# A hybrid attention trunk on one core: context rows, denominators and key preparation moved within a pair of heads

## Chip, cores and metric

The kernel runs on one NeuronCore of a Trainium2 chip. The metric is the device time of one execution in microseconds (us). TensorE is written PE, VectorE DVE, ScalarE ACT, GpSimd POOL, SyncE SP.

## What is computed

One inference step of a two-layer backbone over 128 context tokens and 512 latent tokens, together T = 640 columns. Each layer normalises its input, modulates it, projects it, and gives it to three mixers: A (grouped-query attention, 8 heads), B (latent attention with compressed keys and a rope part, 8 heads), C (a linear scan). Each mixer's output is multiplied by a gate, projected, merged and projected out. The change touches A and B alone. What they compute, cut from the reference:

```python
def _block_attention(q, k, v):
    s = jnp.einsum('bqkgd,bskd->bkgqs', q_blk, k) * scale
    p = jax.nn.softmax(s, axis=-1)
    return jnp.einsum('bkgqs,bskd->bqkgd', p, v)

ya = _block_attention(q, k, v) * jax.nn.silu(a_z)
yb = _mla_attend(qb, ckv, b_kr, lp) * jax.nn.silu(b_z)
```

Context tokens attend to the 128 context tokens. Latent tokens attend to 512 latent and 128 cached keys.

## The kernel before

All matrices are float32. Where accuracy asks for it, an operand is split into a high part (ACT copies it to a rounded type) and a low part (DVE subtracts; POOL does it for weights during the attention), and a product becomes two or three matmuls. `split` (L163, L164) does this for every tile; so its lines stand for many operations, told apart by tile names.

In each layer the stage before the attention runs mixer C with the first projections; the stage behind it merges the three branches (`merge`, products `pm` at L178 to L180) and projects out. The attention works through eight pairs of heads, 0 to 3 of A and 4 to 7 of B. For one pair:

- `context` (L911 on): scores `scc` of the 128 context rows for both heads (L920), maximum, exponential into `Pc` with the row sums.
- `head` for each of the two heads. Scores: for each of four query tiles, `sc` (L958), a maximum `nm` (L961), an exponential `P` (L963) whose row sums go to `rsum`. Values: for each of five key tiles, four transposes `pp` of P (L973), the split into `ph` and `pl`, two products into `po` (L977, L978). Then `finish` adds the two halves of `po` into `OT`: a copy on ACT (L908), an addition on DVE (L909).
- `context2`: transposes `ppc` of `Pc`, split, products `poc` (L939, L940), `finish`.
- `pair_out` (L982 on): reciprocal `ri` of the row sums (L987), broadcast `rib` on POOL (L989), five transposes `pri` (L993), `OT` times `pri` on DVE reading PSUM (L995), `OT` times the gate tile `z` on POOL (L996), and the store (L997).

Meanwhile `pump` advances a generator, `stream(i)`, 18 times in a pair, by a rate from the hand-written table `PLAN`, and `drain` plays the rest of it at the pair's end. The stream prepares the next pair (for B: `b_pair` with queries `QT` and, for every second pair, the projection of the rope queries; `b_pair2` with the rope queries `QR`, transposes `pqr` at L1149, and the values `VS`, products `pvb`; `b_head` with the keys `KH`, `KL` of one head, products `pkh`) and holds the projection of this pair's `z` (`gate_z`, products `pcm` at L225 to L227, 48 for a tile unless it was made earlier and is loaded) and gate projections that are left over (`units`). Before the change, the keys of the second head of a B pair are made at the start of that pair, ahead of its stream.

PSUM has two score buffers of two banks each (tag `S`, also used by `pkh`), two banks of tag `pt` (`pp`, `scc`, `ppc`, `pri`), one of `po` and one of `f`. The tile framework inserts the semaphores and orders the instructions of each engine ahead of time (`schedule_with_timeline_sim=True`): program order is its priority, and what it finds ready earlier may go ahead. Each engine then executes its own list in order. SP issues all loads and stores in its own order.

Of the kernel before, what the change touches and what calls it, by code (L numbers as in the profile page):

```python
# [20 lines left out]
KT = 8  # L21
# [86 lines left out]
class Trunk:  # L108
# [834 lines left out]
    def head(self, e, h, ps, rate):  # L943

        V, S, PE, sm, split, ap = self.V, self.S, self.PE, self.sm, self.split, self.ap
        ident = self.ident
        kq, VS = e.keys[h], e.VS(h)
        OT, rsum = e.OT, e.rsum


        Ps = []
        for qt in range(4):
# [13 lines left out]
            self.pump(rate)  # L966


        po = ps.tile([128, 512], F32, tag="po", name="po")
        for t in range(5):  # L970
            p = ps.tile([128, 512], F32, tag="pt", name="pp")
            for qt in range(4):
                PE.transpose(p[:, qt * 128:(qt + 1) * 128], Ps[qt][:, t * 128:(t + 1) * 128], ident)  # L973
            ph = ap.tile([128, 512], F32R, tag="ph", name="ph", bufs=2)
            pl = ap.tile([128, 512], F32R, tag="pl", name="pl", bufs=2)
            split(ph, pl, p)
            PE.matmul(po, lhsT=VS[:, 1 + t, :], rhs=ph, start=(t == 0), stop=False)  # L977
            PE.matmul(po, lhsT=VS[:, 1 + t, :], rhs=pl, start=False, stop=(t == 4))  # L978
            self.pump(rate)
        self.finish(po, h, OT[:, 128:640])  # L980

    def pair_out(self, e, dst, ps):  # L982

        V, PE = self.V, self.PE
        OT = e.OT
        ri = self.sm.tile([128, 10], F32, tag="ri", name="ri")
        V.reciprocal(out=ri, in_=e.rsum.rearrange("p t h -> p (t h)"))  # L987
        rb = self.tq([128, 5, 2, 64], "rib")
        self.G.tensor_copy(out=rb.rearrange("p t h d -> p (t h) d"), in_=ri.unsqueeze(2).to_broadcast([128, 10, 64]))  # L989
        for t0, n in ((0, 4), (4, 1)):  # L990
            p = ps.tile([128, 512], F32, tag="pt", name="pri")
            for j in range(n):
                PE.transpose(p[:, j * 128:(j + 1) * 128], rb[:, t0 + j].rearrange("p h d -> p (h d)"), self.ident)  # L993
            ts_ = slice(t0 * 128, (t0 + n) * 128)
            V.tensor_tensor(out=OT[:, ts_], in0=OT[:, ts_], in1=p[:, 0:n * 128], op=ALU.mult)  # L995
        self.G.tensor_tensor(out=OT, in0=OT, in1=e.z, op=ALU.mult)  # L996
# [8 lines left out]
    def a_keys(self, l, wp, gp, ps, fill):  # L1005
# [5 lines left out]
        self.KT = KTt = self.kp.tile([128, 2, 2, 768], F32R, tag="KT", name="KT")  # L1011
# [21 lines left out]
        for j, src in enumerate((f32(khr), klo)):  # L1033
            for t0, n in ((0, 4), (4, 2)):
# [3 lines left out]
                for g in range(2):  # L1038
                    for c in range(2):
                        S.copy(out=KTt[c * 64:c * 64 + 64, g, j, t0 * 128:(t0 + n) * 128],  # L1040
# [584 lines left out]
```

## Time and profile before

| | us |
|---|---|
| median of 3 runs | 2320.77 |
| lowest and highest | 2318.45, 2337.36 |
| the profiled execution | 2325.66 |
| its span, first to last instruction | 2323.9 |

The profile is of one execution. Its durations sum to the span, and the execution's own time is 1.8 us longer. In rows of a timeline the first number is the start in us from the span's start and the second the duration in us. A bracket at a row's end holds the engine's idle time just before it and what ended it. A row of windows gives the stretch, its width, the busy time of PE, PEld, DVE, ACT and POOL with the number of instructions, PEclk, the DMA share and GB/s. PEld is PE's weight loading. PEclk is the granted share of the TensorE clock: 1.00 is 2.4 GHz, 0.50 is 1.2 GHz, and a value between them is the mean over a stretch.

### The profile page before, as it was taken

How to read it: one execution, taken by the hardware profiler on the slowest of the kernel's cores; microseconds unless marked ns; L12 is line 12 of the kernel's file. 1: busy time of each engine (PE TensorE's matmuls, PEld its weight loads, DVE VectorE, ACT ScalarE, POOL GpSimd, SP SyncE). 2: the span in 40 equal slices, each digit the busy share in tenths (PEclk: the TensorE clock that was granted, in tenths of full speed). 3: DMA queues.
4: the chain of work that ended last, by engine and by line, in shares of the span. 5: the costliest groups of instructions: out<-in, count | busy, mean ns of one | idle time of the engine just before them, and what ended most of it. 6: DMA issues, size and time to landing. Idle time of an engine off the chain costs nothing.

```text
span 2323.9 us, 40367 instructions
## 1 busy us (share of the span) xinstructions
PE 2130.8 (92%) x15380; PEld 2016.8 (87%) x15380; DVE 1589.3 (68%) x3062; ACT 1108.1 (48%) x2462; POOL 690.2 (30%) x761
## 2 busy tenths in 40 slices
PE   8899998999789889989989999999898889999898
PEld 6889998998789778879988999999898777888898
DVE  4676877867845676775648668668677568667673
ACT  4444443544443666662354444434443447667333
POOL 3332527335233221102033133253352332210011
PEclk9999989989899999999999999899797999999899
DMA  6232222222223311126612322222123231110562
GB/s 227 77 102 77 78 73 95 73 93 84 88 91 109 100 38 52 39 77 192 200 53 74 102 73 79 76 94 76 58 74 99 67 101 46 46 55 24 174 191 83
DMA packets 111762, 209.70 MB, mean 90 GB/s; under 512 B 14416, under 2 KB 33488, under 8 KB 111568
## 3 DMA queue, kind: packets, MB, share of 16 engines
q1 hardware_dynamic: 111568, 207.12, 28.1%
q8 instruction: 121, 1.98, 0.4%
q14 instruction: 73, 0.60, 0.1%
HBM read 163.52 MB, written 43.55 MB: 89 GB/s over the span
## 4 chain that ended last, share of the span: by engine, by line
PE 65%; DVE 18%; ACT 7%; DMA 4%; issue 4%; POOL 2%; DVEq 0%; SPq 0%; ACTq 0%; POOLq 0%
PE pcm L225 10%; PE pcm L226 10%; PE pcm L227 10%; PE sc L958 3%; PE sca L767 2%; PE pm L178 2%; PE pm L179 2%; PE pm L180 2%; DVE wlo L175 2%; PE pA L611 2%; PE pp L973 2%; PE px L679 1%; DVE nm L961 1%; PE scb L782 1%; ACT whi L174 1%
## 5 line engine op out<-in xcount | busy, mean ns | idle before, releaser
L225 PE MATMUL pcm<-hh,whi 128*128 128x320 f32 x1952 | 636.0, 326 | 21.7 <-DVE modc L252 6.7
L227 PE MATMUL pcm<-hh,wlo 128*128 128x320 f32 x1952 | 626.1, 321 | 13.7 <-DVE wlo L175 13.6
L226 PE MATMUL pcm<-hl,whi 128*128 128x320 f32 x1952 | 625.9, 321 | 0.0
L225 PEld LDWEIGHTS pcm<-hh,whi 128*128 128x128 f32 x1952 | 381.3, 195 | 29.4 <-DVE modc L252 7.9
L227 PEld LDWEIGHTS pcm<-hh,wlo 128*128 128x128 f32 x1952 | 380.2, 195 | 18.0 <-DVE wlo L175 16.9
L174 ACT CAST whi<-wraw 128x512 fp32r<-128x512 f32 (+1 forms) x356 | 226.6, 666 | 331.3 <-PE pcm L226 122.0
L226 PEld LDWEIGHTS pcm<-hl,whi 128*128 128x128 f32 x1952 | 381.5, 195 | 1.5
L175 DVE TENSOR_TENSOR wlo<-wraw,whi 128x512 fp32r<-128x512 f32 (+1 forms) x262 | 224.4, 871 | 95.1 <-ACT whi L174 91.3
L175 POOL TENSOR_TENSOR wlo<-wraw,whi 128x512 fp32r<-128x512 f32 x94 | 124.1, 1337 | 195.1 <-ACT whi L174 171.1
L778 POOL COPY ubd<-VZ 64x128 f32<-64x128 f32 x160 | 68.0, 425 | 328.1 <-ACT VZ L775 291.1
L164 DVE TENSOR_TENSOR pl<-pp,ph 128x512 fp32r<-128x512 f32 x160 | 108.4, 685 | 47.8 <-ACT ph L163 46.7
L178 PE MATMUL pm<-yh,whi 128*128 128x320 f32 x384 | 121.7, 317 | 7.1 <-DVE OT L995 3.0
L163 ACT CAST ph<-pp 128x512 fp32r<-128x512 f32 x160 | 92.4, 587 | 64.5 <-PE pp L973 53.9
L961 DVE TENSOR_REDUCE nm<-sc 128x1 f32<-128x640 f32 x128 | 104.4, 818 | 25.0 <-PE sc L958 23.6
L179 PE MATMUL pm<-yl,whi 128*128 128x320 f32 x384 | 121.3, 316 | 0.0
L180 PE MATMUL pm<-yh,wlo 128*128 128x320 f32 x384 | 121.0, 315 | 0.0
L963 ACT ACTIVATE P<-sc,nm 128x640 f32<-128x640 f32 x128 | 102.0, 798 | 18.7 <-DVE nm L961 14.4
L973 PE MATMUL pp<-small,P 128*128 128x128 f32 x640 | 102.2, 280 | 7.2 <-ACT P L963 4.3
L973 PEld LDWEIGHTS pp<-small,P 128*128 128x128 f32 x640 | 80.9, 144 | 24.9 <-ACT P L963 5.3
L611 PE MATMUL pA<-L,BK 128*128 128x128 f32 x640 | 90.7, 285 | 11.4 <-ACT AB L616 7.8
L767 PE MATMUL sca<-VZ,L 128*128 128x64 f32 x640 | 93.3, 285 | 7.7 <-DVE VZ L799 7.6
L996 POOL TENSOR_TENSOR OT<-OT,z 128x640 f32<-128x640 f32 x16 | 27.8, 1736 | 239.7 <-DVE OT L995 216.2
(375 smaller groups left out, 5021.6 us busy)
## 6 DMA issues: line engine op xcount, KB each, us to landing
wraw<-in_win SPq DMA_DIRECT2D x156, 256.0 KB, 2.9
wraw<-in_wg SPq DMA_DIRECT2D x96, 256.0 KB, 3.1
wraw<-in_wmod SPq DMA_DIRECT2D x64, 256.0 KB, 2.9
gsp<-gt SPq DMA_DIRECT2D x48, 320.0 KB, 3.1
gt<-gsp SPq DMA_DIRECT2D x48, 320.0 KB, 3.4
wraw<-in_wo SPq DMA_DIRECT2D x24, 512.0 KB, 4.4
cm<-gsl SPq DMA_DIRECT2D x26, 320.0 KB, 2.5
wraw<-in_wmod SPq DMA_DIRECT2D x16, 512.0 KB, 6.5
```

The costliest lines, as they stand in the source:

```text
L174: self.S.copy(out=hi[part], in_=raw)
L175: sub.tensor_tensor(out=lo[part], in0=raw, in1=f32(hi[part]), op=ALU.subtract)
L178: self.PE.matmul(out, lhsT=lh, rhs=rh, start=first, stop=False)
L179: self.PE.matmul(out, lhsT=lh, rhs=rl, start=False, stop=False)
L180: self.PE.matmul(out, lhsT=ll, rhs=rh, start=False, stop=last)
L225: PE.matmul(p[0:m, 0:H], lhsT=wh[:, kt], rhs=self.hh[:, kt, rs], start=(kt == 0), stop=False)
L226: PE.matmul(p[0:m, 0:H], lhsT=wh[:, kt], rhs=self.hl[:, kt, rs], start=False, stop=False)
L227: PE.matmul(p[0:m, 0:H], lhsT=wl[:, kt], rhs=self.hh[:, kt, rs], start=False, stop=(kt == KT - 1))
L611: PE.matmul(pA[:, j * 128:(j + 1) * 128], lhsT=BK[:, u].rearrange("p a s -> p (a s)"), rhs=L1[h][:, u].rearrange("p a s -> p (a s)"), star ...
L767: PE.matmul(a4[:, d, h], lhsT=L1[h][:, uu[d]].rearrange("p a s -> p (a s)"), rhs=VZ[h][:, cc[d], :], start=(h == 0 and d == 0), stop=False ...
L961: V.tensor_reduce(out=nm, in_=sc[:, :, 0:H], axis=AX.XY, op=ALU.max, negate=True)
L973: PE.transpose(p[:, qt * 128:(qt + 1) * 128], Ps[qt][:, t * 128:(t + 1) * 128], ident)
```

## The change

- `head` becomes `scores` and `values`. `context2` now stands between the scores and the values of the first head. The reciprocals with `rib` and the `pri` transposes become `denominators`, which stands between the scores and the values of the second head and copies `pri` to an SBUF tile `RB` on ACT.
- `values` issues the transposes and the split of key tile t + 1 ahead of the products of tile t.
- `pair_out` is left with two products over all 640 columns and the store; for the last pair both are on DVE.
- In the stream, `b_pair2` and `b_head` for both heads stand right behind `b_pair`, ahead of `gate_z` and of the units, with two more `yield`. `PLAN` is unchanged.
- The keys of A become two tiles, and `KH`, `KL` one tile; they share four buffers of one size.

```diff
-    def head(self, e, h, ps, rate):
+    def scores(self, e, h, ps, rate):
...
+        return Ps
+
+    def values(self, e, h, Ps, ps, rate):
+        PE, ap, VS = self.PE, self.ap, e.VS(h)
+        def turn(t):
+            p = ps.tile([128, 512], F32, tag="pt", name="pp")
+            for qt in range(4):
+                PE.transpose(p[:, qt * 128:(qt + 1) * 128], Ps[qt][:, t * 128:(t + 1) * 128], self.ident)
...
+            self.split(ph, pl, p)
+            return ph, pl
+        nxt = turn(0)
         po = ps.tile([128, 512], F32, tag="po", name="po")
         for t in range(5):
...
+            ph, pl = nxt
+            if t < 4:
+                nxt = turn(t + 1)
             PE.matmul(po, lhsT=VS[:, 1 + t, :], rhs=ph, start=(t == 0), stop=False)
             PE.matmul(po, lhsT=VS[:, 1 + t, :], rhs=pl, start=False, stop=(t == 4))
             self.pump(rate)
...
+    def denominators(self, e, ps):
         ri = self.sm.tile([128, 10], F32, tag="ri", name="ri")
...
+        e.RB = self.ap.tile([128, T], F32, tag="RB", name="RB")
         for t0, n in ((0, 4), (4, 1)):
...
-            V.tensor_tensor(out=OT[:, ts_], in0=OT[:, ts_], in1=p[:, 0:n * 128], op=ALU.mult)
-        self.G.tensor_tensor(out=OT, in0=OT, in1=e.z, op=ALU.mult)
+            self.S.copy(out=e.RB[:, t0 * 128:(t0 + n) * 128], in_=p[:, 0:n * 128])
+
+    def pair_out(self, e, dst, last):
+        OT = e.OT
+        self.V.tensor_tensor(out=OT, in0=OT, in1=e.RB, op=ALU.mult)
+        (self.V if last else self.G).tensor_tensor(out=OT, in0=OT, in1=e.z, op=ALU.mult)
         self.nc.sync.dma_start(out=dst, in_=OT)
...
-        self.KT = KTt = self.kp.tile([128, 2, 2, 768], F32R, tag="KT", name="KT")
+        self.KT = KTt = [self.kp.tile([128, 2, 768], F32R, tag="KT", name="KT", bufs=4) for _ in range(2)]
...
-        KH = ap.tile([128, 768], F32R, tag="KH", name="KH", bufs=2)
-        KL = ap.tile([128, 768], F32R, tag="KL", name="KL", bufs=2)
+        KHL = self.kp.tile([128, 2, 768], F32R, tag="KT", name="KHL", bufs=4)
+        KH, KL = KHL[:, 0], KHL[:, 1]
...
                 elif i < 7:
                     e = yield from self.b_pair(l, i - 3, wp, gp, ps)
+                    self.b_pair2(l, e, ps)
+                    yield
+                    self.b_head(l, e, 0, ps)
+                    yield
+                    self.b_head(l, e, 1, ps)
                 yield from self.gate_z(es[i], l, W_AZ if i < 4 else W_BZ, wp, ps)
-                yield from units(n // 2)
-                if 3 <= i < 7:
-                    self.b_pair2(l, e, ps)
-                    self.b_head(l, e, 0, ps)
-                yield from units(n - n // 2 if i < 7 else len(gates))
+                yield from units(n if i < 7 else len(gates))
                 return e
...
             for i in range(8):
-                if i > 3:
-                    self.b_head(l, es[i], 1, ps)
                 self.stream = stream(i)
-                rate = self.plan.rates[i] / 18
-                self.context(es[i], ps)
-                for h in range(2):
-                    self.head(es[i], h, ps, rate)
-                self.context2(es[i], ps)
+                rate, e = self.plan.rates[i] / 18, es[i]
+                self.context(e, ps)
+                Ps = self.scores(e, 0, ps, rate)
+                self.context2(e, ps)
+                self.values(e, 0, Ps, ps, rate)
+                Ps = self.scores(e, 1, ps, rate)
+                self.denominators(e, ps)
+                self.values(e, 1, Ps, ps, rate)
                 e = self.drain()
                 if e:
                     es.append(e)
-                self.pair_out(es[i], self.ysp[i // 4][i % 4], ps)
+                self.pair_out(es[i], self.ysp[i // 4][i % 4], i == 7)
```

## Rows read from the trace of the kernel before

**Rows 1.** The page's part 1, busy time by engine, share of span, instructions

```profile
PE 2130.8 (92%) x15380; PEld 2016.8 (87%) x15380; DVE 1589.3 (68%) x3062; ACT 1108.1 (48%) x2462; POOL 690.2 (30%) x761
```

**Rows 2.** Windows over the two attention stretches: one per layer

```profile
773.90:1047.00 273.10, 248.11 (x1524) 215.86 (x1525) 202.22 (x377) 181.10 (x413) 47.08 (x39) 0.95 0.16 52
1891.70:2172.00 280.30, 253.74 (x1582) 224.30 (x1583) 202.59 (x385) 184.14 (x420) 50.90 (x42) 0.95 0.18 56
```

**Rows 3.** Windows around pair ends of layer 0, and the sum with layer 1's three

```profile
901.50:924.00 22.50, 17.95 (x93) 15.59 (x92) 14.86 (x25) 15.59 (x38) 1.54 (x1) 0.77 0.11 39
950.00:962.00 12.00, 9.88 (x58) 8.78 (x57) 10.16 (x22) 9.90 (x25) 6.13 (x5) 0.89 0.09 33
1040.00:1047.00 7.00, 3.77 (x18) 3.13 (x18) 4.83 (x9) 2.68 (x6) 1.78 (x1) 0.84 0.04 7
...
sum 84.00, PE 64.40 PEld 55.99 DVE 60.63 ACT 56.81 POOL 19.14; mean PE 10.73 PEld 9.33 DVE 10.11 ACT 9.47 POOL 3.19
```

**Rows 4.** PE's timeline from the end of pair 3 into pair 4, layer 0

```profile
894.41 0.41 PE L225 MATMUL pcm<-hh,whi 128*128 128x320 f32 x1
...
897.88 0.31 PE L227 MATMUL pcm<-hh,wlo 128*128 128x320 f32 x1
...
903.85 0.40 PE L978 MATMUL po<-pl,VS 128*128 128x512 f32 x1
...
905.65 0.30 PE L1149 MATMUL pqr<-small,qr 128*64 128x128 f32 x1 [0.85 <-DVE QR L1156]
...
920.35 0.44 PE L973 MATMUL pp<-small,P 128*128 128x128 f32 x2 [1.55 <-ACT P L963]
...
922.41 0.39 PE L977 MATMUL po<-ph,VS 128*128 128x512 f32 x1
```

**Rows 5.** Windows inside that change, and over pair 3 ahead of it

```profile
908.30:918.50 10.20, 9.87 (x41) 9.12 (x42) 4.40 (x8) 5.09 (x15) 1.54 (x1) 0.50 0.07 24
...
874.00:901.50 27.50, 27.02 (x183) 25.31 (x182) 17.07 (x42) 15.93 (x36) 8.88 (x8) 1.00 0.25 78
```

**Rows 6.** Tile pkh: ns min/median/max, first and last start us

```profile
L178 PE MATMUL pkh<-KB,uk x32: 334/339/522, 869.0 to 2116.2; 128*128 128x384 f32 x32
```

**Rows 7.** Timeline behind the last product of pair 7, layer 0

```profile
1040.30 0.50 PE L978 MATMUL po<-pl,VS 128*128 128x512 f32 x1 [0.23 <-DVE pl L164]
...
1041.45 0.69 DVE L909 TENSOR_TENSOR OT<-po,ot 64x512 f32<-64x512 f32 x1 [0.77 <-ACT ot L908]
...
1042.19 0.33 PE L939 MATMUL poc<-pch,VS 128*128 128x128 f32 x1 [0.85 <-DVE OT L909]
...
1043.30 0.33 PE L939 MATMUL poc<-pch,VS 128*128 128x128 f32 x1 [0.67 <-DVE OT L909]
...
1045.22 2.01 POOL L996 TENSOR_TENSOR OT<-OT,z 128x640 f32<-128x640 f32 x1 [15.79 <-DVE OT L995]
1045.23 0.61 PE L178 MATMUL pm<-yh,whi 128*128 128x320 f32 x1 [1.49 <-DVE OT L995]
```

**Rows 8.** Groups by line and shape: xcount | busy us, mean ns | idle before

```profile
L896 ACT COPY q<-pqt 128x512 f32<-128x512 f32 x8 | 4.7, 583 | 1.4 <-PE pqt L895 1.3
...
L1053 DVE TENSOR_TENSOR q<-q,qrb 128x640 f32<-128x640 f32 x8 | 6.6, 822 | 11.5 <-POOL qrb L237 11.4
```

**Rows 9.** POOL's timeline in pair 3, layer 0

```profile
877.33 0.72 POOL L989 COPY rib<-ri 128x640 f32<-128x640 f32 x1 [12.31 <-DVE ri L987]
```

**Rows 10.** Groups by line of PE, attention of layer 0 (columns as above)

```profile
L978 PE MATMUL po<-pl,VS 128*128 128x512 f32 x80 | 35.7, 446 | 3.9 <-DVE pl L164 3.6
...
L977 PE MATMUL po<-ph,VS 128*128 128x512 f32 x80 | 34.8, 434 | 2.5 <-ACT ph L163 2.0 <-DVE OT L909 0.3
```

**Rows 11.** ACT's timeline at the change from pair 3 to pair 4, layer 0

```profile
916.95 0.59 ACT L1154 ACTIVATE QR<-pqr 32x512 fp32r<-32x512 f32 x1 [0.63 <-PE pqr L1149]
917.55 0.58 ACT L1155 ACTIVATE QR<-pqr 32x512 fp32r<-32x512 f32 x1
918.15 0.80 ACT L163 CAST KH<-pkh 128x768 fp32r<-128x768 f32 x1
```

More of the change, by code (lines that the diff above doesn't have):

```diff
@@ L941, in context2 @@
             self.finish(po[:, hs], h, e.OT[:, 0:128])
-    def head(self, e, h, ps, rate):
[L945 to L948, printed above, removed]
+    def scores(self, e, h, ps, rate):
+        V, S, PE, sm, ap = self.V, self.S, self.PE, self.sm, self.ap
+        kq, rsum = e.keys[h], e.rsum
         Ps = []
@@ L966, in head @@
             self.pump(rate)
+        return Ps
[5 more added lines that the diff above has]
+                PE.transpose(p[:, qt * 128:(qt + 1) * 128], Ps[qt][:, t * 128:(t + 1) * 128], self.ident)
+            ph = ap.tile([128, 512], F32R, tag="ph", name="ph", bufs=2)
+            pl = ap.tile([128, 512], F32R, tag="pl", name="pl", bufs=2)
+            self.split(ph, pl, p)
+            return ph, pl
+        nxt = turn(0)
         po = ps.tile([128, 512], F32, tag="po", name="po")
         for t in range(5):
[L971 to L976, printed above, removed]
+            ph, pl = nxt
+            if t < 4:
+                nxt = turn(t + 1)
             PE.matmul(po, lhsT=VS[:, 1 + t, :], rhs=ph, start=(t == 0), stop=False)
@@ L979, in head @@
             self.pump(rate)
[L980 to L985, printed above, removed]
+        self.finish(po, h, e.OT[:, 128:640])
+    def denominators(self, e, ps):
         ri = self.sm.tile([128, 10], F32, tag="ri", name="ri")
-        V.reciprocal(out=ri, in_=e.rsum.rearrange("p t h -> p (t h)"))
+        self.V.reciprocal(out=ri, in_=e.rsum.rearrange("p t h -> p (t h)"))
         rb = self.tq([128, 5, 2, 64], "rib")
         self.G.tensor_copy(out=rb.rearrange("p t h d -> p (t h) d"), in_=ri.unsqueeze(2).to_broadcast([128, 10, 64]))
+        e.RB = self.ap.tile([128, T], F32, tag="RB", name="RB")
         for t0, n in ((0, 4), (4, 1)):
@@ L1039, in a_keys @@
                     for c in range(2):
-                        S.copy(out=KTt[c * 64:c * 64 + 64, g, j, t0 * 128:(t0 + n) * 128],
+                        S.copy(out=KTt[g][c * 64:c * 64 + 64, j, t0 * 128:(t0 + n) * 128],
                                in_=p[g * 64:g * 64 + 64, 0:n * 128])
@@ L1066, in a_pair2 @@
             self.split_q(QT, slice(t0 * 128, (t0 + n) * 128), p[:, 0:n * 128])
-        e.keys = [[(QT[:, h], self.KT[:, g, 0]), (QT[:, h], self.KT[:, g, 1])] for h in range(2)]
+        e.keys = [[(QT[:, h], self.KT[g][:, 0]), (QT[:, h], self.KT[g][:, 1])] for h in range(2)]
         e.VS = lambda h: self.VSa[:, :, g, :]
```

3 lines of the change are left out of this document (1 added, 2 removed).

## The prediction

> **What bounds the kernel now.** The page comes first: TensorE (PE) is busy 92% of the span [rows 1]. The change touches only the attention, so the next view is the windows over its two stretches, one per layer: 273.1 and 280.3 us, with PE busy 248.1 and 253.7 us, DVE 202 and ACT 181 to 184 [rows 2]. PE is the bound there, and what a change of order can give back is PE's lost time: idle 25.0 + 26.6 = 51.6 us, and the clock. The windows' mean of 0.95 means that 5% of 553.4 us, 27.7 us, went by at the lower level. Together 79 us, a ceiling that no reordering passes.
>
> Where it is lost is read from windows laid around the changes of pair in layer 0, and their sum with layer 1 [rows 3]:
> - from pair 3 (the last of branch A) to pair 4 (the first of branch B): 22.5 us with PE busy 17.95 and a clock of 0.77; idle 4.55, clock 0.23 x 22.5 = 5.18, so 9.7 lost;
> - from pair 4 to pair 5: 2.12 idle + 0.11 x 12 = 1.32 clock, 3.4 lost;
> - behind pair 7: 3.23 + 0.16 x 7 = 1.12, 4.35 lost.
> For both layers, doubled: 19.5, 6.9 and 8.7, together 35 us. The sum row of the six windows agrees: 84.0 - 64.4 = 19.6 idle, against 2 x 9.9 here. So nearly half of the 79 us lies at three of the eight pair ends.
>
> The timeline shows why the first is so dear. The last product of pair 3 starts at 903.85, the first of pair 4 at 922.41: 18.6 us apart [rows 4]. In between PE waits 0.85 us for the rope queries of pair 4 (QR) and 1.55 us for its softmax rows (P), and from 908.3 to 918.5 it runs at 1.2 GHz (granted clock 0.50) although it had 1.00 while it was fed, from 874 to 901.5 [rows 5]. Pair 4's queries are prepared too late.
>
> **The change, part by part.** The program's order is not the order on the engines: the keys of pair 4's heads are multiplied from 869.0 on, before pair 3 begins [rows 6]. Program order acts as a rank among what is ready. So what counts is which late item now ranks earlier.
>
> 1. Preparation of a B pair. b_pair2 (QR, values) and both b_head now stand before the gate tile z, not behind it and, for the second head, behind the change. No instruction is added; per pair 5 transposes, 18 + 12 products, ACT's and DVE's part of them and three weight loads on the SP queue move up. The two ukr loads share one buffer, so on SP the second waits for the split of the first, with z's weights queued behind it. That costs nothing to 1.55 us a time by the longest wait in [rows 4]; I take 0, since z is wanted only at the pair's end. What is gained: the second half of z, 24 products, ran from 894.41 to 898.0 [rows 4], so a whole z holds PE for 7.2 us. Ranked ahead of it, QR can be finished near 898 instead of 905.65, scores of pair 4 fall under pair 3's products, and z's products are left as cover. If the hole closes, the 19.5 us go; if half of its idle part alone goes, 4.6. QR's 7 us against an 18.6 us hole, of which PE spends more than half on work that it only does slowly, is nearer the upper end: 16. From pair 4 to pair 5 nothing or all of 6.9 may go; the second head's keys are out of the way there, but P is not: 4.5.
>
> 2. Tail of the layer. Now PE waits 0.85 us for OT behind the last product, multiplies the context in two steps, 0.67 between them, and the merge waits 1.49 for the scaled OT: 1040.30 to 1045.23 [rows 7]. Afterwards context and denominators are done earlier, and what stays is the last product (0.50), a copy (0.58 by the ACT row of [rows 8]) and the addition that frees po (0.69), about 2 us with their gaps. Of 8.7 lost some 3.2 remain: 5.5 saved; bounds 0 and 8.7. The last product with z goes from POOL (2.01 us) to DVE (0.82) [rows 7, 8]; the store leaves 1.2 us earlier, hidden, because this branch is merged last.
>
> 3. Denominators. Two DVE multiplications that read PSUM become two ACT copies (0.58, and at most that for the short one) and one DVE product of 0.82 [rows 8]. ACT gets at most 16 x 1.17 = 18.7 us; it is busy 181 of 273 us, which hides it; without that cover it is 18.7. The broadcast rib was early already: 877.33 for pair 3, whose change is at 902 [rows 9]; so reciprocals and rib gain nothing. But pri now stands between the two heads' work on PE, and whatever is ranked behind it there waits with it: the second head's transposes. Per pair 0 to the 2.01 us of one product on POOL that could stand before rib; with 25 us of room seen, I take 0.1, in 16 pairs 2 us lost.
>
> 4. Transposes one tile ahead. PE's products wait for the splits ph and pl 3.9 + 2.5 us in layer 0 [rows 10], some 12.8 in both. Transposes ran ahead already where PE was free, so I take 2.5 saved; bounds 0 and 12.8.
>
> 5. New collisions: the pkh of both heads take score banks while scores run, and two more steps use up the stream's rates, which are unchanged. Bounds 0 and 8 x 1.55 = 12 by the wait for P in [rows 4]; I take 2 lost.
>
> Sum: 16 + 4.5 + 5.5 + 2.5 - 2 - 2 = 24.5 us. The profiled execution took 2325.66 us (span 2323.9 and 1.8 around it), 0.21% over the median of 2320.77. 2325.66 - 24.5 = 2301.2; by the same ratio 2296 us on the median's scale, 1.1% less.
>
> **The rivals.**
> A. The clock does not come back. If small waits remain, the windows give their idle shares alone: 9.1 of 19.5, 4.2 of 6.9, 6.5 of 8.7. With the fractions taken above (0.82, 0.65, 0.63): 7.5 + 2.7 + 4.1 + 2.5 - 4 = 12.8, time 2308. For it: the clock fell at 908.3 with no wait over 0.85 us ahead of it in [rows 4]. Against: the 1.00 from 874 to 901.5, PE busy 27.0 of 27.5 us.
> The Trainium skill speaks for A: TensorE: Matmul & The Clock Gate, section "A second HAM failure mode: psum-queue depth-cycling", says that frequent short idling between groups of matmuls, not only one long wait, makes the clock swing between its levels. The 0.50 behind short waits agrees. By that rule thinner stalls would not pay twice, and the sum would be A's.
>
> B. The hole moves instead of closing. The engines' order looked far ahead already, and ACT and DVE keep the same work; then the tail's 5.5 us are all: 2315. For it: nothing is taken away from any engine. Against: ACT at 66% and DVE at 74% of the stretch leave room.
>
> C. Slower. The preparation, ranked higher, stands on ACT in front of the pair's own softmax rows. For one pair ACT has at least QR 2 x (0.59 + 0.58) and KH 2 x 0.80 = 3.9 us; at 916.95 to 918.95 QR and KH are seen to run on ACT while PE waits for P [rows 4, 11]. If all of it stood in PE's way in each of the eight preparations, 31 us would be lost against 24.5 won: 2327. It decides from 24.5 / 8 = 3.1 us per preparation. Against: in the trace such a bunch cost 1.55.
>
> D. Better. All the lost time of the six windows but 4 us goes, and two thirds of part 4's bound with it: 31 + 8.5 = 39.5, time 2281.
>
> **How the numbers follow.** Forecast 0.36, A 0.18, B 0.15, C 0.11, D 0.20. A measurement of this kernel can tell about 1%, 23 us, from no change; the border is 2297.6, almost the forecast: half of its chance, D's and a little of A's lie below it, so faster 0.45, same 0.47, and slower 0.08 (C with larger bunches, over 2344, and what is not listed). The range cuts off D's lower third and C's upper half: 2274 to 2326.
>
> **What would show it.** Right: from pair 3's last product to pair 4's first under 10 us instead of 18.6, with a clock near 1.00, in both layers; each stretch shorter by about 12 us and the rest of the kernel unchanged; merge products within 3 us of pair 7's last product; pri between the heads without a wait. Wrong: stretches shorter by less than 5 us each (B), a clock still at 0.95 over them (A), waits of PE for P and pl grown beyond today's (C).

## The result, and the profile after

The changed kernel takes 2311.6 us (median of 20 runs, 2305.0 to 2320.3) against 2326.2 us (20 runs, 2310.8 to 2343.6) for the kernel before on the same chips: a ratio of 0.9938, with a 95% interval of [0.9919, 0.9957]. That is 0.6% or 14.6 us, where 24.5 us (1.1%) were forecast. The direction is right; the size is 10 us short. The profiled execution took 2311.49 us with a span of 2309.8.

Page part 1 after the change, answering to [rows 1]:

```profile
PE 2118.7 (92%) x15380; PEld 2005.6 (87%) x15380; DVE 1584.5 (69%) x3048; ACT 1116.8 (48%) x2494; POOL 686.3 (30%) x759
```

No matmul was added or taken away (15380 in both); they ran 12 us shorter, so the clock is part of the gain. From here on the attention of a layer is measured between two fixed marks, its first context score (`scc`) and its 96th merge product (`pm`), so that the kernels can be compared: "attention" is the sum of both layers, "rest" is the rest of the span. First windows of the kernel before, then of the kernel after: attention of layer 0, what lies between, attention of layer 1.

```profile
773.90:1058.80 284.90, 259.91 (x1600) 227.66 (x1601) 208.87 (x387) 183.52 (x416) 47.31 (x39) 0.95 0.19 59
1058.80:1891.70 832.90, 771.24 (x5743) 752.89 (x5741) 569.12 (x1104) 349.06 (x769) 271.01 (x317) 0.93 0.29 92
1891.70:2183.70 292.00, 265.44 (x1654) 236.00 (x1655) 208.41 (x395) 186.66 (x423) 50.90 (x42) 0.95 0.20 63
```

```profile
770.30:1042.90 272.60, 250.91 (x1601) 219.61 (x1602) 203.55 (x377) 188.44 (x432) 44.23 (x38) 0.98 0.19 59
1042.90:1885.90 843.00, 779.64 (x5742) 761.10 (x5741) 569.78 (x1107) 348.98 (x769) 273.74 (x317) 0.92 0.29 92
1885.90:2169.60 283.70, 256.55 (x1654) 227.61 (x1655) 207.10 (x385) 190.72 (x439) 47.13 (x41) 0.98 0.20 61
```

The attention is 12.3 and 8.3 us shorter, 20.6 together. The stretch between, whose code the change does not touch, is 10.1 us *longer*. (Its instructions are the same ones, but not all in the same order: the two traces list PE's 5739 matmuls there with 382 places that differ, all of them between 1216 and 1365 us.) And within the attention the idle time of PE (width less PE busy) went only from 25.0 + 26.6 to 21.7 + 27.2 us; what came back is the clock, 0.95 to 0.98.

At the changes of pair, though, the idle time did go. Windows of the kernel after at the places of [rows 3], layer 0, then the one of layer 1 that kept most, and the sum:

```profile
903.20:925.70 22.50, 20.82 (x146) 19.66 (x145) 15.87 (x28) 16.19 (x38) 4.73 (x4) 1.00 0.19 56
943.80:955.80 12.00, 11.32 (x77) 9.97 (x75) 7.22 (x19) 8.28 (x18) 4.89 (x5) 1.00 0.09 33
1030.10:1037.10 7.00, 6.78 (x46) 6.70 (x46) 4.13 (x7) 2.69 (x4) 0.00 (x0) 1.00 0.34 92
2014.50:2037.00 22.50, 19.80 (x128) 18.81 (x129) 15.38 (x28) 14.25 (x37) 0.00 (x0) 0.92 0.09 24
...
sum 84.00, PE 78.40 PEld 73.63 DVE 55.08 ACT 52.19 POOL 13.78; mean PE 13.07 PEld 12.27 DVE 9.18 ACT 8.70 POOL 2.30
```

Idle in these six windows fell from 19.6 to 5.6 us (84.0 - 78.4), and of the 15.2 us that the clock took there (twice the layer's 5.18 + 1.32 + 1.12) only 0.08 x 22.5 = 1.8 is left: 27.4 us recovered at the very places where 26 were forecast. So outside these windows the idle time rose from 51.6 - 19.6 = 32.0 to 48.9 - 5.6 = 43.3 us. About half of this rise is at the other five changes of pair, from the last product of one pair to the first of the next (3.9 to 9.3 us), the rest inside the pairs.

The change from pair 3 to pair 4 looks as the prediction drew it. PE's timeline there, answering to [rows 4]:

```profile
902.07 0.46 PE L954 MATMUL sc<-KHL,QT 128*128 128x320 f32 x2
...
905.62 0.45 PE L985 MATMUL po<-pl,VS 128*128 128x512 f32 x1
...
907.38 0.39 PE L225 MATMUL pcm<-hh,whi 128*128 128x320 f32 x1
...
919.82 0.48 PE L984 MATMUL po<-ph,VS 128*128 128x512 f32 x1
```

Pair 4's scores start ahead of pair 3's last product (905.62), and z's products fill in behind it. The distance from last to first product is still 14.2 us (18.6 before), but it holds work at full clock. And the tail, answering to [rows 7]: the merge goes on 0.34 us after the last product, where it was 4.93. (In both kernels the first 12 of the layer's 96 merge products run earlier, under pair 7.)

```profile
1030.36 0.50 PE L985 MATMUL po<-pl,VS 128*128 128x512 f32 x1 [0.23 <-DVE pl L164]
1030.70 0.30 PE L178 MATMUL pm<-yh,whi 128*128 128x320 f32 x1
```

What rose is the waits of the products, layer 0, answering to [rows 10]: `pl` 3.6 to 5.1, `ph` 2.0 to 2.6, and `OT` (the one `po` bank, free once the addition into `OT` has read it) 0.3 to 1.8 us. `pri`, last, waits for nothing; what waits 1.1 us in each layer is the second head's transposes behind it, for the ACT copy into `RB`.

```profile
L984 PE MATMUL po<-ph,VS 128*128 128x512 f32 x80 | 37.2, 466 | 4.5 <-ACT ph L163 2.6 <-DVE OT L909 1.8
L985 PE MATMUL po<-pl,VS 128*128 128x512 f32 x80 | 35.3, 442 | 5.1 <-DVE pl L164 5.1
...
L999 PE MATMUL pri<-small,rib 128*128 128x128 f32 x40 | 7.3, 288 | 0.0
```

### The profile page after: what moved, and what is told of

The parts are those of the page before. It is cut to its first block, busy times and chain, and to the rows that moved or that the text cites. A ratio compares the mean times of both kernels' runs of the same rounds, so it can differ in the third digit from the quotient of the medians.

```text
span 2309.8 us, 40379 instructions
## 1 busy us (share of the span) xinstructions
PE 2118.7 (92%) x15380; PEld 2005.6 (87%) x15380; DVE 1584.5 (69%) x3048; ACT 1116.8 (48%) x2494; POOL 686.3 (30%) x759
## 4 chain that ended last, share of the span: by engine, by line
PE 60%; DVE 19%; ACT 9%; DMA 6%; issue 5%; POOL 1%; SPq 0%; DVEq 0%; ACTq 0%; POOLq 0%
PE pcm L225 9%; PE pcm L226 9%; PE pcm L227 9%; PE sc L954 3%; PE sca L767 3%; DVE wlo L175 2%; PE pA L611 2%; PE pm L179 2%; PE pm L180 2%; PE pm L178 2%; ACT whi L174 2%; DVE BK L547 2%; PE pp L972 1%; PE sca L786 1%; PE px L679 1%
## 5 line engine op out<-in xcount | busy, mean ns | idle before, releaser
L164 DVE TENSOR_TENSOR pl<-pp,ph 128x512 fp32r<-128x512 f32 x160 | 107.1, 685 | 25.5 <-ACT ph L163 24.2
L611 PE MATMUL pA<-L,BK 128*128 128x128 f32 x640 | 92.6, 288 | 13.8 <-ACT AB L616 9.8
L767 PEld LDWEIGHTS sca<-VZ,L 128*128 128x128 f32 x640 | 94.2, 216 | 9.9 <-DVE VZ L799 9.2
L972 PE MATMUL pp<-small,P 128*128 128x128 f32 x640 | 97.4, 276 | 2.7 <-ACT RB L1000 2.2
L611 PEld LDWEIGHTS pA<-L,BK 128*128 128x128 f32 x640 | 84.4, 201 | 17.3 <-ACT AB L616 11.7
```

The source lines that it names most:

```text
L164: self.V.tensor_tensor(out=lo, in0=src, in1=f32(hi), op=ALU.subtract)
L611: PE.matmul(pA[:, j * 128:(j + 1) * 128], lhsT=BK[:, u].rearrange("p a s -> p (a s)"), rhs=L1[h][:, u].rearrange("p a s -> p (a s)"), star ...
L767: PE.matmul(a4[:, d, h], lhsT=L1[h][:, uu[d]].rearrange("p a s -> p (a s)"), rhs=VZ[h][:, cc[d], :], start=(h == 0 and d == 0), stop=False ...
```

## Experiments

### The parts alone

**Preparation alone.** The kernel before, with `b_pair2` and both `b_head` ahead of `gate_z`, and with the four key buffers that this needs:

```diff
                     e = yield from self.b_pair(l, i - 3, wp, gp, ps)
+                    self.b_pair2(l, e, ps)
+                    yield
+                    self.b_head(l, e, 0, ps)
+                    yield
+                    self.b_head(l, e, 1, ps)
```

> The kernel before with one part of the change alone: b_pair2 and both b_head ahead of z and of the units (with the two yields and the four key buffers). Theory S (the parts add up, the preparation gives, the transposes ahead cost): the change from pair 3 to pair 4 closes, 12 to 20 us less than before, ratio 0.9915 to 0.995; after's extra PE waits for ph and pl (5.6 to 7.7 us in layer 0, 4.7 to 8.7 in layer 1) do not appear. Rival N (the parts don't add, every reordering scatters the waits anew): ratio 0.995 to 1.000, waits for ph and pl as in after.

Measured: 0.993 [0.991, 0.995], 2307.1 us. Attention 555.1 us. Theory S holds: at the change from pair 3 to pair 4 PE is idle 0.1 us between the last and the first product instead of 3.1, and its products wait 5.5 us for `pl` and 2.0 for `ph` in both layers together. What the four buffers alone give was not tried.

**Transposes ahead alone:**

```diff
+            ph, pl = nxt
+            if t < 4:
+                nxt = turn(t + 1)
```

> The kernel before with the transposes and split of key tile t + 1 ahead of the products of tile t, alone. Theory S: 4 to 8 us slower than before, ratio 1.002 to 1.0035, PE's waits for ph and pl grow by 4 us or more over both layers. Rival N and the prediction's part 4: no loss, ratio 0.998 to 1.000.

Measured: 0.9947 [0.9926, 0.9967], 2313.8 us, attention 566.5. Theory S falls, and so does rival N: this part was taken for 2.5 us in the sum and gains 12 by itself.

**Context rows and denominators alone:**

```diff
                 Ps = self.scores(e, 0, ps, rate)
+                self.context2(e, ps)
                 self.values(e, 0, Ps, ps, rate)
                 Ps = self.scores(e, 1, ps, rate)
+                self.denominators(e, ps)
                 self.values(e, 1, Ps, ps, rate)
```

> The kernel before with the context rows and the denominators moved (RB copied by ACT, one DVE product, the last pair's z product on DVE), alone. Theory S: only the tails gain, 4 to 9 us, ratio 0.996 to 0.998. Rival N: the new places cost as much as the tails give, ratio 0.999 to 1.002; PE waits for OT ahead of po and for RB appear.

Measured: 1.0053 [1.0033, 1.0072]: 2335.8 us, slower than either theory had it. PE's waits for the `po` bank in layer 0 rose from 0.3 [rows 10] to 6.1 us:

```profile
L981 PE MATMUL po<-ph,VS 128*128 128x512 f32 x80 | 35.7, 446 | 7.3 <-DVE OT L909 6.1 <-ACT ph L163 1.2
```

The three parts alone give -16, -12 and +12 us by their ratios. Their sum, -16, lies within the noise of the whole change (-14.6), but that is chance: taken two at a time, in the next two runs, they do not add.

### One part taken out of the change

**Without the transposes ahead:**

```diff
         for t in range(5):
-            ph, pl = nxt
-            if t < 4:
-                nxt = turn(t + 1)
+            ph, pl = turn(t)
```

> The changed kernel without the transposes ahead (each tile's transposes again stand right before its products). Theory S: 4 to 8 us faster than the changed kernel, ratio to before 0.990 to 0.992, PE's waits for ph and pl back near 5 us a layer. Rival N: as the changed kernel, 0.993 to 0.995.

Measured: 0.9949 [0.9925, 0.9972], attention 562.7. Theory S falls again. The two parts that are left give -12 us together, where -16 and +12 alone would make -4. By the time the change does not need the transposes ahead; by the trace they shorten its attention by 8.2 us (562.7 to 554.5, the mean of its three profiles below).

**Without the moves of context rows and denominators**, which stand behind the second head's values again, `pair_out` as before:

```diff
-                self.context2(e, ps)
                 self.values(e, 0, Ps, ps, rate)
                 Ps = self.scores(e, 1, ps, rate)
-                self.denominators(e, ps)
                 self.values(e, 1, Ps, ps, rate)
+                self.context2(e, ps)
```

> The changed kernel without the move of the context rows and without the move of the denominators (both as before, at the pair's end); the preparation and the transposes ahead stay. Theory C (the two early parts cost about as much as the tails give or more, preparation and transposes ahead each give): faster than the changed kernel by 6 to 14 us, ratio to before 0.987 to 0.991. Rival V (preparation and transposes ahead fill the same holes, so together they give no more than the better one): ratio 0.992 to 0.995.

Measured: 0.9946 [0.9926, 0.9966], attention 555.8. Rival V holds: preparation and transposes together gain no more than the preparation alone, -12.6 us instead of -28.

### The two moves apart, and variants of them

**Context back at the pair's end, denominators early:**

```diff
                 Ps = self.scores(e, 0, ps, rate)
-                self.context2(e, ps)
...
                 self.values(e, 1, Ps, ps, rate)
+                self.context2(e, ps)
```

> The changed kernel with context2 back behind the values of the second head; denominators stay early. Theory C1 (the context products hold the one po bank ahead of the first head's products): PE's waits of po for OT go from 3.1 us over both layers to under 1, 3 to 8 us faster than the changed kernel, though the tails lose 2 to 3 us each; ratio 0.990 to 0.993. Theory C2 (the denominators are the cost): as the changed kernel, 0.993 to 0.996.

Measured: 1.0041 [1.0023, 1.0059], attention 578.9, worse than either theory had it, and 0.010 worse than the change.

**Context early, denominators back in `pair_out`:**

```diff
-                self.denominators(e, ps)
                 self.values(e, 1, Ps, ps, rate)
...
+            V.tensor_tensor(out=OT[:, ts_], in0=OT[:, ts_], in1=p[:, 0:n * 128], op=ALU.mult)
```

> The changed kernel with the denominators back in pair_out, read from PSUM by DVE, the z product of every pair on POOL; context2 stays early. Theory C2 (the denominators' ACT copies and the transposes waiting for them are the cost): 3 to 8 us faster than the changed kernel, PE's waits for RB (2.2 us over both layers) gone; ratio 0.990 to 0.993. Theory C1: as the changed kernel or slower, 0.993 to 0.997.

Measured: 1.0147 [1.0104, 1.019], attention 613.9, the slowest of all. Here `pri` keeps the `pt` banks until `OT` is multiplied at the end of the pair, and the next pair's first context scores wait for a `pt` bank, 4.4 us in layer 0. It is a wait for the multiplication (L1002), and was 0.4 us at most in a layer before:

```profile
L920 PE MATMUL scc<-KHL,QT 128*128 128x128 f32 x16 | 3.0, 279 | 4.4 <-DVE OT L1002 4.4
```

This wait, 8.3 us in both layers, is only a part of the loss: against the full change PE's idle time in the attention is 25 us more (74.0 against 48.7), and the lower clock takes 44.8 us instead of 8.4, in a profile that is one of the slowest of this kernel's runs. With the context early, `scc`, `Pc`, `ppc`, the split and `poc` stand ahead of a pair's first products, and a late `scc` delays all of them; that is read from the program and was not tested. Each move without the other is worse than both together (554.5) and than neither (555.8): with the context early, the denominators have to be early too.

**The copies into `RB` on DVE instead of ACT:**

```diff
-            self.S.copy(out=e.RB[...], in_=p[:, 0:n * 128])
+            self.V.tensor_copy(out=e.RB[...], in_=p[:, 0:n * 128])
```

> The full change with the copies of pri into RB on DVE instead of ACT. Theory R (the ACT copies between the heads delay exponentials and high parts, part of what ate the gain): PE's waits for ph and P in the stretches fall from 4.5 and 2.6 us a layer by 2 us or more together, ratio 0.990 to 0.993. Rival S (the wait is for the order on PE and its PSUM banks, not for ACT; DVE is the busier engine and its low parts pl wait more): waits for pl grow from 5.1 to 6 to 8 us a layer, ratio 0.994 to 0.998.

Measured: 0.9975 [0.9959, 0.9991]. In rival S's range, but not by its reason: over both layers PE waited 9.9 us for `pl` (12.2 in the change) and 15.2 us for `P` at the scores (9.9 in the change). Both theories missed which wait would move. So the change does not get faster when ACT is rid of the copies.

**Context between the scores and the values of the second head:**

```diff
-                self.context2(e, ps)
                 self.values(e, 0, Ps, ps, rate)
                 Ps = self.scores(e, 1, ps, rate)
+                self.context2(e, ps)
                 self.denominators(e, ps)
```

> The full change with context2 between the scores and the values of the second head, ahead of the denominators. Theory C (the context's products hold the one po bank ahead of the first head's products, and so delay the first head): PE's waits for OT at the products fall from 1.8 us a layer to under 0.8 without another growing, ratio 0.988 to 0.992. Rival Q (context, denominators and the transposes of the second head then all queue for the two pt banks at one place): waits for pl or for pt's readers grow by 3 us or more a layer, ratio 0.996 to 1.004, between the full change and the one with the context at the pair's end (1.004).

Measured: 0.9958 [0.9942, 0.9974], between the two theories and no faster than the full change. The wait for the `po` bank ahead of the heads' products fell from 3.1 to 2.1 us in both layers, and the context's own products waited 5.8 us for it instead: the bank's price moved.

### The last pair and the other seven

**Context and denominators moved in the last pair alone, on the kernel before:**

```diff
+                if i == 7:
+                    self.context2(e, ps)
                 self.values(e, 0, Ps, ps, rate)
...
+                if i == 7:
+                    self.denominators(e, ps)
```

> The kernel before with the context rows and denominators moved in the last pair alone (and that pair's product with z on DVE). Theory T (the tail is a term of its own): the first merge product starts within 1 us of pair 7's last product in both layers instead of 4.9 us, PE's idle time in the two stretches falls from 51.6 by 4 to 6 us, and the ratio to the kernel before is 0.997 to 0.9985. Theory K (what the other variants gained is the clock, which returns with any change of the order): clock lost in the two stretches falls from 27.7 to under 18 us here too, and the ratio is 0.993 to 0.996.

Measured: 0.9949 [0.9928, 0.9969], attention 563.6. The merge goes on 0.34 us behind the last product in both layers, and PE's idle time in the attention fell by 5.7 us, as T had it; the time fell by more, as K had it, although the clock took 20.2 us, over K's limit of 18. Neither theory holds whole.

**The same with the early preparation** (both edits together):

> The early preparation of the B pairs, with context rows and denominators moved in the last pair alone; the other seven pairs in the order of before, transposes not ahead. Theory T (terms 1 and 2 of the sum are right and add, and what ate them is context and denominators in the other seven pairs): the ratio of the preparation alone, 0.993, less the tail's 0.0024: 0.988 to 0.992, faster than the full change's 0.994. Rival O (as with the preparation and the transposes together, the parts overlap): 0.9925 to 0.9955, no faster than the full change.

Measured: 0.9926 [0.9903, 0.9949], 2304.6 us: just inside rival O's range, and its interval reaches into T's.

Then four kernels side by side on one chip. The preparation with the last pair's move once more, and the full change once more:

> The early preparation with context rows and denominators moved in the last pair alone, once more, beside the full change on one chip. Theory T (the first seven pairs' moves cost the full change some 7 us): 2300 to 2306 us, at least 0.002 below the full change's ratio. Rival O (all variants with the early preparation end at one level): within 0.002 of the full change's ratio.

> The full change, a third time: 0.992 to 0.996 as in the two series before. It is the yardstick for the other three runs of this call.

Measured: 2296.8 us, 0.9894 [0.9874, 0.9914], against 2310.8 us, 0.9955 [0.9938, 0.9972] for the full change. The intervals do not meet: **this version beats both kernels**, the full change by 14.0 us here. T's order holds; the time is even below its range. In the earlier series the medians were 7 us apart (2304.6 and 2311.6), with intervals that did meet. Its attention, 274.2 + 275.8 = 550.0 us (548.8 in its first profile):

```profile
774.20:1048.40 274.20, 252.65 (x1601) 221.54 (x1602) 206.23 (x384) 185.08 (x418) 45.00 (x38) 0.97 0.18 58
...
1881.50:2157.30 275.80, 255.59 (x1655) 227.65 (x1655) 205.33 (x392) 187.82 (x425) 48.06 (x41) 0.98 0.19 62
```

**Moved in the first seven pairs alone, on the kernel before:**

```diff
-                if i == 7:
+                if i < 7:
                     self.context2(e, ps)
...
-                if i == 7:
+                if i < 7:
                     self.denominators(e, ps)
```

> The kernel before with context rows and denominators moved in the first seven pairs alone (the last pair as before). Theory T (moved everywhere they measured 1.0053, and in the last pair alone 0.9949, so the loss is in the first seven): ratio 1.005 to 1.012, slower than both, PE's idle time in the two stretches over 58 us. Rival L (the loss of the move everywhere lies at the last pair too, and the gain of the last pair alone was the clock's): 1.000 to 1.004.

Measured: 1.0063 [1.0041, 1.0086], with PE idle 30.5 + 30.6 = 61.1 us (from the widths and busy times below). T holds for the ratio and the idle time; that it is slower than with the last pair moved too (1.0053 [1.0033, 1.0072]) is not clear of the noise:

```profile
777.40:1066.10 288.70, 258.22 (x1600) 226.18 (x1601) 210.98 (x380) 187.41 (x430) 48.55 (x39) 0.95 0.18 59
...
1892.50:2185.70 293.20, 262.54 (x1652) 233.11 (x1653) 211.50 (x385) 190.31 (x437) 49.74 (x41) 0.97 0.19 60
```

**The full change with these seven pairs as before:**

```diff
+                if i == 7:
                     self.context2(e, ps)
...
+                if i == 7:
                     self.denominators(e, ps)
                 self.values(e, 1, Ps, ps, rate)
+                if i < 7:
+                    self.context2(e, ps)
```

> The full change without the moves of context rows and denominators in the first seven pairs (preparation, transposes ahead and the last pair as in the full change). Theory T (these moves are what ate the gain): 0.988 to 0.992, some 7 us under the full change, PE's idle time under 46 us. Rival O (with preparation and transposes together there is nothing left to win, as 0.9946 for the two without the tail): 0.993 to 0.996.

Measured: 0.9933 [0.9907, 0.9959], 2307.6 us, so by the time O. By the trace T: the attention is the shortest of all, 269.3 + 276.8 = 546.1 us, PE idle 41.1. Its rest was 1755.6 us, 8 more than in the profile of the version without the transposes ahead. All of that lies ahead of the first attention (784.6 us against 774.2), where the two programs run the same, and the intervals of the two times still meet (0.9907 and 0.9914); so the time decides little here. The two stretches, and then the waits in layer 0, first of this kernel, then of the full change on the same chip:

```profile
784.60:1053.90 269.30, 250.95 (x1600) 221.26 (x1601) 203.31 (x384) 183.29 (x418) 44.48 (x38) 0.98 0.18 60
...
1884.50:2161.30 276.80, 253.99 (x1655) 226.03 (x1655) 208.23 (x392) 187.86 (x425) 47.92 (x41) 0.99 0.19 62
```

```profile
L972 PE MATMUL pp<-small,P 128*128 128x128 f32 x320 | 50.0, 280 | 2.9 <-DVE pl L164 2.5 <-ACT RB L1000 0.4
L984 PE MATMUL po<-ph,VS 128*128 128x512 f32 x80 | 36.9, 461 | 1.8 <-ACT ph L163 1.5 <-DVE OT L909 0.3
L985 PE MATMUL po<-pl,VS 128*128 128x512 f32 x80 | 34.7, 434 | 4.4 <-DVE pl L164 4.3
```

```profile
L972 PE MATMUL pp<-small,P 128*128 128x128 f32 x320 | 48.2, 274 | 1.7 <-ACT RB L1000 1.4 <-ACT P L959 0.2
L984 PE MATMUL po<-ph,VS 128*128 128x512 f32 x80 | 36.2, 453 | 4.6 <-ACT ph L163 2.7 <-DVE OT L909 1.8
L985 PE MATMUL po<-pl,VS 128*128 128x512 f32 x80 | 34.6, 432 | 6.1 <-DVE pl L164 6.0
```

With the moves in all pairs the products wait 10.7 us (4.6 + 6.1) instead of 6.2, spread over `ph`, `pl` and the `po` bank; 1.2 us of this the transposes `pp` wait less. In layer 1 the context's transposes wait for `Pc` on top, 4.1 us there and none in the kernel without the moves:

```profile
L932 PE MATMUL ppc<-small,Pc 128*128 128x128 f32 x16 | 4.4, 318 | 4.4 <-ACT Pc L925 4.1 <-DVE QR L1167 0.3
```

### The same kernels again

**The full change once more**, without an edit:

> The changed kernel itself once more, as the yardstick on this chip and for a second profile. If the clock's return in the attention belongs to the change, its two stretches again lose 8 to 14 us to the lower clock (before: 29.7); if it was chance, 15 to 30. Ratio 0.992 to 0.996.

Measured: 0.9942 [0.9922, 0.9962], 2312.0 us, with 8.1 us lost to the lower clock: it belongs to the change.

**The kernel before, profiled twice more**, without an edit:

> The kernel before, profiled once more. Theory E (the rest of the kernel, unchanged, loses more clock behind the changed attention): attention stretches 575 to 579 us together, the rest 1745 to 1749 us. Rival W (the rest scatters from run to run by its half-clock stretches): the rest lies more than 4 us off 1747.

> The kernel before, profiled a third time, same expectation: Theory E attention stretches 575 to 579 us together and the rest 1745 to 1749 us; Rival W the rest more than 4 us off 1747 here or in the run before.

Measured: attention 574.9 and 568.4, rest 1744.4 and 1755.4 us; the second is off by more than 4 us in both directions, so E falls for the sum and W holds. But the part between the two attentions agrees with E. All six profiles, in us (clock: half of the time at a granted 0.50 within the attention, by the trace's clock records):

| | attention | its idle PE | its clock | ahead of it | between | behind it |
|---|---|---|---|---|---|---|
| before | 576.9 | 51.6 | 29.7 | 773.9 | 832.8 | 140.2 |
| before, 2nd | 574.9 | 51.1 | 28.6 | 771.1 | 833.0 | 140.2 |
| before, 3rd | 568.4 | 53.3 | 18.3 | 779.3 | 835.9 | 140.2 |
| after | 556.3 | 48.9 | 10.2 | 770.3 | 843.0 | 140.2 |
| after, 2nd | 553.8 | 48.5 | 8.1 | 774.6 | 842.5 | 139.9 |
| after, 3rd | 553.5 | 48.7 | 6.8 | 770.4 | 839.9 | 141.1 |

The means: attention 573.4 to 554.5, -18.9 (idle -3.3, clock 25.5 to 8.4 = -17.1, and 1.5 more in the products); between +7.9; ahead -3.0 and behind +0.2; together -13.8, close to the 14.6 us by the medians.

The places of [rows 3] differ between the profiles of the kernel before. PE's idle time in the six windows is 19.6, 19.8 and 21.6 us, but the clock takes 15.7, 10.7 and 3.2 us there; after the change it is 5.6, 4.0 and 4.0 us idle and 1.7, 0 and 0 for the clock. So by the means 25.1 us came back at these places, 15.8 idle and 9.3 clock, while the idle time outside them rose by 12.5 us. The forecast had taken the clock's price from the profile in which it was highest. In the third profile, at the change from pair 3 to pair 4 of layer 0, PE is idle for 5.5 us and the clock stays up, where [rows 3] had 0.77:

```profile
907.00:929.50 22.50, 16.96 (x115) 14.65 (x114) 18.31 (x30) 18.03 (x45) 1.56 (x1) 1.00 0.11 39
```

The part between can be followed to one place, the scan of mixer C in layer 1. From the first `px` to the next projection `pcm` it takes 45.64 us before (47.9 and 49.3 in the other two profiles) and 52.39 us after (52.4 in both others), with PE's instructions in the same order. Windows of the kernel before over the stretches of lower clock there and the one behind, and of the kernel after:

```profile
1771.80:1795.70 23.90, 20.49 (x212) 19.46 (x213) 13.01 (x29) 6.78 (x24) 7.72 (x12) 0.50 0.13 43
1795.70:1806.00 10.30, 6.48 (x45) 5.41 (x43) 3.35 (x13) 2.76 (x11) 3.14 (x10) 1.00 0.02 6
```

```profile
1757.50:1801.90 44.40, 37.33 (x283) 34.86 (x284) 19.73 (x48) 11.53 (x40) 12.25 (x27) 0.50 0.11 35
```

PE's timeline of the kernel before and of the kernel after, the first `px` and the next `pcm`:

```profile
1772.16 4.10 PE L679 MATMUL px<-NF,AB 32*32 32x32 f32 x80 [0.76 <-DVE NF L670]
...
1817.80 0.41 PE L225 MATMUL pcm<-hh,whi 128*128 128x320 f32 x1 [0.57 <-ACT vn L896]
```

```profile
1759.24 4.10 PE L679 MATMUL px<-NF,AB 32*32 32x32 f32 x80
...
1811.63 0.63 PE L225 MATMUL pcm<-hh,whi 128*128 128x320 f32 x1 [0.46 <-ACT vn L896]
```

Both fall to 1.2 GHz at about the same place; before the change the clock is back after 23.9 us (in all three profiles), after it only after 44.4 us (in all three).

## Why the prediction was wrong in size

The attention by steps, each a difference of two profiles or means of profiles from above. They lead from the kernel before to the kernel after, one part at a time in this order; since the parts do not add, another order gives other terms, and the ranges stand behind the table:

| step | attention | difference | forecast |
|---|---|---|---|
| before (3 profiles) | 573.4 | | |
| + preparation early (1) | 555.1 | -18.3 | -16 - 4.5 + 2 = -18.5 |
| + context, denominators, last pair (2) | 549.4 | -5.7 | -5.5 |
| + transposes ahead (1) | 546.1 | -3.3 | -2.5 |
| + context, denominators, other seven pairs: after (3) | 554.5 | +8.4 | +2 |

A row of one profile is uncertain by some us: the attention of before spans 8.5 us in its three, that of the two with the preparation and the last pair 1.2. Each part can be read from four pairs of kernels above that differ in it alone: the preparation gives -18.3 to -10.7 us of attention, the last pair's move -9.8 to -2.9, the transposes ahead -8.2 to +0.7, the move in the other seven pairs +8.4 to +15.4.

- **Part 1 (preparation) and part 5 (collisions): right in size, in part by luck.** The hole of pair 3 closed as described. But of the 18.3 us only 4.9 are idle time and 13.6 clock, where the forecast's fractions had some 10 of each: new waits came elsewhere, for the `po` bank 5.1 us instead of 0.3 in both layers, and the kernel before loses 10.2, 6.8 and 0 us to the clock at the two changes from pair 3 to pair 4 in its three profiles. The rows that reach it are the scores of pair 4 under pair 3's products. The sign that I named, under 10 us from last to first product, was wrong though: that distance is 14.2 us in layer 0 and 19.9 to 23.0 in layer 1, filled with work, mainly z's products in layer 0. The window's idle time and clock are the sign, not a distance.
- **Part 2 (tail): right** in the chain, and alone by its idle time (-5.7 us; the attention is 9.8 us shorter there). The prediction took the 1.49 us in [rows 7] for a wait for the scaled `OT`. By the program those merge products read branch C, not `OT`; the DVE product that ended the wait (L995) is the last reader of a PSUM bank of `pri`, so the bank is the likelier reason, and it was not tested. The move of the last product to DVE was not tried by itself.
- **Part 4 (transposes ahead): right within what one profile can tell** as the third step, but not a constant. Alone it gave 12 us; with the preparation nothing (0.9946 against 0.993); on top of preparation and last pair the attention is 3.3 us shorter, while the time was 10.8 us longer on one chip (2307.6 against 2296.8, intervals that meet); in the full change it shortens the attention by 8.2 us. What it is worth in time stays open.
- **Part 3 (context and denominators): the step that failed.** It was priced at 2 us in all, and this price was for the denominators: the broadcast `rib` was early, so `pri` would not wait, and only the transposes behind it might. That came out: `pri` waits 0.0, the transposes 2.2 us for `RB` in both layers. But the context's products moved too, in front of the first head's, and for the seven pairs in which something follows the sum has no term for that: it was put at nothing without a reason.

  The moves in the first seven pairs cost 8.4 us in the full change, 581.9 - 573.4 = 8.5 us on the kernel before, and more in the other two settings: 15.4 us (579.0 against 563.6, with the last pair moved) and 13.3 us (562.7 against 549.4, with preparation and last pair). In all four PE's idle time rises, by 7.6 to 15.4 us. In all four PE waits for the context's `Pc`, 2.4 to 3.6 us more than without the moves, and for `RB`, 1.4 to 1.5 us more. The other waits change from setting to setting: that for the `po` bank ahead of the heads' products rises by 5.4 us on the kernel before, but by 1.2 in the full change, and the preparation alone has 5.1 us of it and is fast. So in the full change the bank is a small part of the price at most. How much belongs to the context and how much to the denominators was not separated, since each move without the other is worse than both. Nor was it shown whether the `pt` banks or the order on ACT and DVE decide.
- **"The rest of the kernel unchanged": failed too.** Its instructions are unchanged, its order on PE and its time are not: 7.9 us longer between the attentions, most of it (4.8 us of means, 52.4 against 47.6) in layer 1's scan at the lower clock. By the profiles' means 24.5 - 13.8 = 10.7 us are missing: 6.4 of part 3 and 5.1 of the rest, less 0.8 that the other three steps gave more. The cause of the 5.1 stays open.

Of the rivals, A's time (2308) lies nearest to the measured ratio on the forecast's scale, 2320.77 x 0.9938 = 2306.4, and its mechanism is the opposite of what happened. It had the clock stay away and the idle time go; over the whole attention the idle time stayed (52.0 to 48.7 us) and the clock came back (25.5 to 8.4 us). (In the prediction 27.7 us "went by at the lower level"; that is what the level cost. The time at it was twice as long.) The rule behind it, in the Trainium skill's TensorE: Matmul & The Clock Gate, section "A second HAM failure mode: psum-queue depth-cycling", has frequent short idling make the clock swing. The traces agree with it only in part. Before the change the fall at 908.3 came behind waits of at most 0.85 us; but behind the same waits of 0.85 and 0.48 us the third profile has no fall, and after the change PE's waits of up to 1 us make 35.6 us in the attention instead of 27.7 (means), with the clock at 0.98 to 0.99. What became less is the waits over 1 us, from 22.4 to 11.8 us. B (only the tail) falls by the preparation alone, 0.993. C's sign was half seen, but not by its reason: the products' waits for `pl` grew (7.3 to 12.2 us in both layers), while the preparation alone, which C blames, has 5.5 for `pl` and 7.5 for `P` (9.6 before). Most of the growth is a change of reader: together with the transposes, PE waits 11.7 us for `pl` without the moves in the first seven pairs and 12.9 with them (mean of three). D's time was not reached, though its size in the attention nearly was, 573.4 - 546.1 = 27.3 us, by the kernel without the moves in the first seven pairs.

## What to carry to other kernels

When a group of steps is moved, price each step that moves, and ask of each what bank and which engine it now occupies ahead of work that was first; a move that pays at the last iteration, where nothing follows, can cost at all the others, so test it there alone (here -9.8 us for the last pair and +8.5 for the other seven, each on the kernel before). Judge a change of order by a stretch between two fixed marks and by several profiles of both kernels: here the stretch repeats within 3 us after the change and within 8.5 before it, while code elsewhere that nobody edited moved by 8. A time that agrees with a theory says little for it; idle time and clock have to be looked at apart.

## What was not expected of the hardware

- The same instructions in the same order on the same engine ran 23.9 us at 1.2 GHz in three profiles of one kernel and 44.4 us in three of another, in a part that the two kernels share, more than 700 us behind the code that differs. PE's idle time in it is the same, 9.5 to 9.9 us. The order of the work in this part does not decide: two kernels whose PE, ACT and POOL run one and the same order from the first attention to the second show 23.9 us (preparation and transposes) and 44.4 us (context back at the pair's end), and so do two others (best version 23.9, move in the last pair alone 44.4). Why the clock comes back later is open.
- The first 770 us, with PE's instructions in the same order in all kernels, took 767.9 to 784.6 us in the profiles, with 39.5 to 58.9 us of it lost to the lower clock. The idle time of PE in them stays within 66.4 to 73.7. So a single profile of one kernel says no more than some 10 us about another.
- In the attention the clock's loss does not follow the total of idle time: with the idle total down by 6% (52.0 to 48.7 us), it fell by two thirds. Nor do the same waits always bring the lower clock: at the change from pair 3 to pair 4 of layer 0 the kernel before had 0.77 in two profiles and 1.00 in the third.
